# One decoder layer, its traced instructions ordered by a detailed timeline instead of a simple estimate

## Chip, core and metric

The kernel runs on one core of one Trainium2 chip. The metric is the device time of one execution in microseconds (us); the time before is the median of three runs. One more execution was profiled, and all views come from it. Engines are named as in the profile: PE (TensorE, matrix products; PEld is its loading of weights), DVE (VectorE), ACT (ScalarE), POOL (GpSimd), SP (SyncE, which here only issues DMAs).

## What is computed

One layer of a hybrid decoder in float32, for a prompt of 2048 tokens and for eight sequences of eight new tokens, each with 2048 past positions in a paged cache. The width is 1024, the hidden width of the MLP 2816.

```python
h = rmsnorm(x, norm_mix) * (1 + sc_m) + sh_m           # scales, shifts, gates from silu(c) @ w_ada
rq, rk, rv, rg, sq, sk, sv = split(h @ w_in)           # 1024 -> 3584
# 4 heads of 128, chunks of 128 tokens: retention
o = (q k^T * decay) v + (q * q_decay) s;  s = s * chunk_decay + (k * k_decay)^T v
ro = group_norm(o) * silu(rg)
# 8 heads of 64, strictly causal: stick-breaking attention
A[t, s] = sigmoid(z[t, s]) * prod_{s<j<t} (1 - sigmoid(z[t, j]));  so = rmsnorm(A v)
x = x + g_m * (concat(ro, so) @ w_out)
h = rmsnorm(x, norm_ffn) * (1 + sc_f) + sh_f
ff = (silu(causal_conv3(h @ w_up_gate)) * (h @ w_up_val)) @ w_down
x = x + g_f * ff;  y = rmsnorm(x, norm_final)
```

Outputs are also the new rows of K and V, the retention state and the state of the convolution.

## The kernel before

**Precision and tiles.** Most products are made from a high and a low part in a rounded float32 format, three products for one (`mm3`, lines 295 to 297). So each slab of weights is loaded as float32 (`raw`, two buffers of 1 MB, two slabs to a buffer), copied to its high part by ACT (line 174, `whl<-raw`) and subtracted to its low part by DVE (helper `tt`, line 159, `whl<-raw,whl`). `whl` has six buffers, that is three slabs. Activations stand in `act`, also in two parts. In PSUM there are four buffers `d` for the dense products, three buffers `z` for everything that is short, and one `acc`.

**Work by token blocks.** The prompt is cut into four blocks of 512 tokens; the 64 new tokens ride with block 0 in the projections and with block 3 in the MLP. The parts are Python generators that trace a piece of work and yield an estimate of its cost: `in_block` (normalisation and the projection by `w_in`), `decode` (attention of the new tokens over the pages), `retention`, `attention`, then per block `out_block` (projection by `w_out`) and `ffn_block`. `_weave` traces a step of the generator that is furthest behind by these estimates, so the traced program already mixes the streams: first `in_block` with `decode` and the rest of `w_ada`; then `in_block` with `retention` and the attention of block 0; then the MLPs of blocks 0 to 2 with the attention of blocks 1 to 3; last the MLP of block 3 alone. A change from one block to the next is where `out_block` waits for the block's attention and features are made for the next MLP.

**Steps of attention** (lines 1122 to 1196): `qk` multiplies queries and keys into a `z` buffer (line 1144, `z<-akk,aq`); ACT makes two sigmoids (`aom`, `abe`, lines 1147 and 1148); POOL masks or puts in the carry (lines 1151 to 1158); DVE scans along the keys (line 1161) and multiplies; five steps later `turn` transposes into a `z` buffer (line 1173, `z<-con,abe`), ACT and DVE split it (`ahl`), and a step after that `av` multiplies by the values into `acc` (line 1185). Retention makes scores (line 1015), masks them (`scd`), and its group norm reads a `z` buffer four times by ACT (line 979, `on<-z`) after a chain of small POOL instructions.

**What sets the order on the chip.** Every engine works through one queue in order, and SP issues all 1361 DMAs in one queue. Inside `TileContext` the kernel only traces. When the context closes, a list planner runs the traced instructions on a simulated machine: each time an engine of that machine is free it is given the oldest traced instruction whose inputs and buffers are ready there, and buffers are handed out as they come free there. The order so found is what is compiled, with semaphores for all dependencies. By default the machine is a simple estimate: a duration for each instruction. In the compiled program of before, the four-places-or-more moves against the traced order are 3,275 of 16,670 instructions on PE and 2,347 of 2,386 on SP. In one place the kernel holds the planner back: `tc.issue_after` keeps a page's index load behind the eighth page load before it.

## Time and profile before

| | |
|---|---|
| runs (us) | 3423.82, 3425.92, 3428.62; median 3425.92 |
| profiled execution (us) | 3422.1, of which 3420.4 from the first to the last instruction (the span) |
| mean granted clock of TensorE | 0.986 |
| moved by DMA | 527.72 MB, mean 154 GB/s |

The busy times by engine, the stages and the waits are shown in the prediction, where they are used. A wait's row names the instruction that waited and the one whose end released it, each by engine, written tile and line; a line such as 159 or 174 is that of a helper, and the tile tells which use it is. Matrix products overlap in the records, so a product's listed duration is longer than the distance to the next.

### The profile page before, as it was taken

The page shows a single profiled execution, that of the slowest core. Times are in us where ns is not written, and L with a number is a line of the kernel's source. Part 1 is how long each engine was busy: PE and PEld are TensorE (multiplying, and loading weights), DVE is VectorE, ACT ScalarE, POOL GpSimd, SP SyncE. Part 2 cuts the span into 40 slices and gives each one's busy share as a digit, 9 for nine tenths or more (in the row PEclk, how much of TensorE's full clock was granted, in tenths as well). Part 3 has the DMA queues.
Part 4 walks back from the last instruction along what each step waited for, and adds up shares of the span by engine and source line. Part 5 has one row for each costly group of instructions (what it writes and reads, how often), then busy time and mean ns, then how long its engine had stood idle before and what let it go on. Part 6 is the DMA issues. An engine that isn't in the chain of part 4 may idle for free.

```text
span 3420.4 us, 49521 instructions
## 1 busy us (share of the span) xinstructions
PE 3273.5 (96%) x17111; PEld 2676.8 (78%) x17111; DVE 2287.6 (67%) x3258; ACT 1772.8 (52%) x3153; POOL 1029.1 (30%) x1898
## 2 busy tenths in 40 slices
PE   7999999999988989999998999999899999899998
PEld 5877777776777768878877877877788787799997
DVE  5466666764665567777778777877878774554445
ACT  5457556654544446555556555555655553433223
POOL 3012001101443233433344343334433333221113
PEclk9999999999999999999999999999999999999999
DMA  6765776776656773433464343336333334332221
GB/s 235 234 202 191 235 235 209 239 241 206 198 179 193 243 224 95 126 117 113 123 199 122 117 120 108 118 113 197 118 115 108 114 105 146 106 109 81 81 87 66
DMA packets 406233, 527.72 MB, mean 154 GB/s; under 512 B 27830, under 2 KB 244009, under 8 KB 405982
## 3 DMA queue, kind: packets, MB, share of 16 engines
q1 hardware_dynamic: 405982, 524.55, 49.0%
q8 instruction: 136, 2.23, 0.3%
q14 instruction: 115, 0.94, 0.1%
HBM read 442.47 MB, written 81.99 MB: 153 GB/s over the span
## 4 chain that ended last, share of the span: by engine, by line
PE 45%; DVE 2%; POOL 1%; ACT 1%; issue 1%; DMA 1%; SPq 0%; POOLq 0%; DVEq 0%; ACTq 0%
PE d L295 11%; PE d L296 11%; PE d L297 11%; PE acc L1185 3%; PE z L1144 2%; PE z L1173 2%; PE z L297 1%; PE z L296 1%; PE z L295 1%; DVE whl L159 1%; DVE hf L159 1%; DVE aom L1161 0%; POOL ff L159 0%; ACT whl L174 0%; PE z L304 0%
## 5 line engine op out<-in xcount | busy, mean ns | idle before, releaser
L174 ACT CAST whl<-raw 128x1024 fp32r<-128x1024 f32 x456 | 477.2, 1050 | 940.9 <-PE d L296 661.7
L159 DVE TENSOR_TENSOR whl<-raw,whl 128x1024 fp32r<-128x1024 f32 x456 | 573.9, 1262 | 523.1 <-ACT whl L174 514.2
L295 PE MATMUL d<-act,whl 128*128 128x512 f32 (+2 forms) x2016 | 738.8, 367 | 2.3 <-DVE hf L159 1.4
L297 PE MATMUL d<-act,whl 128*128 128x512 f32 (+2 forms) x2016 | 734.3, 364 | 1.1 <-DVE whl L159 1.1
L296 PE MATMUL d<-act,whl 128*128 128x512 f32 (+2 forms) x2016 | 730.9, 363 | 0.2
L295 PEld LDWEIGHTS d<-act,whl 128*128 128x128 f32 x2016 | 382.7, 190 | 62.4 <-issue 3.1
L297 PEld LDWEIGHTS d<-act,whl 128*128 128x128 f32 x2016 | 382.1, 190 | 60.6 <-DVE whl L159 2.2
L296 PEld LDWEIGHTS d<-act,whl 128*128 128x128 f32 x2016 | 383.5, 190 | 55.9 <-issue 0.4
L295 PE MATMUL d<-whl,ff 128*128 128x512 f32 x704 | 279.3, 397 | 0.0
L296 PE MATMUL d<-whl,ff 128*128 128x512 f32 x704 | 278.9, 396 | 0.0
L297 PE MATMUL d<-whl,ff 128*128 128x512 f32 x704 | 278.3, 395 | 0.0
L295 PE MATMUL d<-whl,act 128*128 128x512 f32 x640 | 257.5, 408 | 5.5 <-ACT whl L174 5.5
L296 PE MATMUL d<-whl,act 128*128 128x512 f32 x640 | 258.8, 404 | 0.3 <-DVE whl L159 0.3
L1161 DVE TENSOR_TENSOR_SCAN aom<-aom,acy 128x512 f32<-128x512 f32 x192 | 256.0, 1333 | 3.1 <-ACT aom L1147 2.4
L297 PE MATMUL d<-whl,act 128*128 128x512 f32 x640 | 257.3, 403 | 0.0
L159 DVE TENSOR_TENSOR abe<-abe,aom 128x512 f32<-128x512 f32 (+2 forms) x320 | 230.1, 719 | 29.9 <-POOL abe L1151 7.9
L1185 PE MATMUL acc<-ahl,avv 128*128 128x512 f32 (+3 forms) x640 | 223.5, 411 | 18.4 <-DVE ahl L159 8.4
L1147 ACT ACTIVATE aom<-z,nb 128x512 f32<-128x512 f32 (+2 forms) x320 | 200.9, 628 | 72.6 <-PE z L1144 50.0
L1148 ACT ACTIVATE abe<-z,bb 128x512 f32<-128x512 f32 (+2 forms) x320 | 199.6, 624 | 0.0
L1144 PE MATMUL z<-akk,aq 128*128 128x512 f32 (+3 forms) x640 | 190.5, 375 | 8.6 <-DVE scd L159 5.9
L159 DVE TENSOR_TENSOR ahl<-z,ahl 128x512 fp32r<-128x512 f32 (+1 forms) x320 | 191.3, 598 | 10.3 <-ACT ahl L174 9.9
L1343 DVE SCALAR_TENSOR_TENSOR c<-a,vecs,c 128x512 f32<-128x512 f32 x176 | 133.3, 759 | 81.8 <-ACT c L1340 47.2
(295 smaller groups left out, 6238.9 us busy)
## 6 DMA issues: line engine op xcount, KB each, us to landing
raw<-in_w_in SPq DMA_DIRECT2D x56, 1024.0 KB
raw<-in_w_up_gate SPq DMA_DIRECT2D x44, 1024.0 KB
raw<-in_w_up_val SPq DMA_DIRECT2D x44, 1024.0 KB
akk<-k SPq DMA_DIRECT2D x160, 256.0 KB
page<-in_cache_k_pages SPq DMA_DIRECT2D x128, 256.0 KB
page<-in_cache_v_pages SPq DMA_DIRECT2D x128, 256.0 KB
raw<-in_w_down SPq DMA_DIRECT2D x32, 1024.0 KB
raw<-in_w_ada SPq DMA_DIRECT2D x24, 1024.0 KB
```

The costliest lines, as they stand in the source:

```text
L159: eng.tensor_tensor(o, a, b, op)
L174: act.copy(hi, src)
L295: pe.matmul(ps, sh, mh, start=start, stop=False)
L296: pe.matmul(ps, sh, ml, start=False, stop=False)
L297: pe.matmul(ps, sl, mh, start=False, stop=stop)
L1144: pe.matmul(z[:, :n], qs[g, h][:, i * P : (i + 1) * P], kk[:, c, :n], start=c == 0, stop=c == 1)
L1147: act.activation(om[:, :n], z[:, :n], AF.Sigmoid, bias=nb[:, h : h + 1], scale=-SCALE)
L1148: act.activation(be[:, :n], z[:, :n], AF.Sigmoid, bias=bb[:, h : h + 1], scale=SCALE)
L1161: dve.tensor_tensor_scan(rv, rv, rv, init, ALU.mult, ALU.bypass)
L1173: pe.transpose(ps[:, i * P : (i + 1) * P], As[u, i][:, kt * P : (kt + 1) * P], ident)
L1185: pe.matmul(accs[0][:, cs], kv[u][1][:, kt, :], m[:, cs], start=(s == g and kt == 0 and c == 0), stop=(s == 0 and kt == NT - 1 and c == 1),)
L1343: dve.scalar_tensor_tensor(c[:, :TB], a[:, j : j + TB], cw(j), c[:, :TB], ALU.mult, ALU.add)
```

## The change

One argument of the context is set. The traced program, the streams, the tiles and the buffers' counts stay as they are. The planner's simulated machine becomes the library's detailed timeline, which follows each instruction through the queue, wait and execution of its engine, and through devices that engines or DMAs share.

```diff
-    with _tile.TileContext(nc) as tc:
+    with _tile.TileContext(nc, schedule_with_timeline_sim=True) as tc:
         body(tc, ins, outs)
```

## The prediction

> **What bounds the kernel now.** I read the page first (busy times, chain of work that ended last), then cut the span into stages with the view of windows, then the waits of TensorE, and last the order of time around single stalls.
>
> ```profile
> span 3420.4 us, 49521 instructions
> PE 3273.5 (96%) x17111; PEld 2676.8 (78%) x17111; DVE 2287.6 (67%) x3258; ACT 1772.8 (52%) x3153; POOL 1029.1 (30%) x1898
> PE 45%; DVE 2%; POOL 1%; ACT 1%; issue 1%; DMA 1%; SPq 0%; POOLq 0%; DVEq 0%; ACTq 0%
> ```
>
> TensorE is the bound: busy for 3273.5 of 3420.4 us, and it heads the chain; DVE follows at 67%. A new order leaves the instructions as they are, so what it can win is the idle 146.9 us of TensorE, and what it can lose is more of the same. Where those lie, by stages (columns: stretch, its length, busy us of PE, PEld, DVE, ACT, POOL with counts, granted clock, DMA share, GB/s):
>
> ```profile
> 0.00:100.00 100.00, 79.23 (x479) 58.37 (x480) 55.49 (x70) 55.55 (x91) 26.88 (x46) 0.93 0.71 237
> 100.00:850.00 750.00, 718.50 (x3865) 572.90 (x3864) 464.94 (x704) 432.35 (x785) 100.85 (x209) 0.98 0.67 221
> 850.00:1330.00 480.00, 434.23 (x2389) 353.70 (x2389) 293.40 (x591) 236.03 (x476) 182.58 (x378) 0.98 0.64 194
> 1330.00:1780.00 450.00, 448.47 (x2121) 360.17 (x2121) 347.39 (x440) 245.51 (x418) 179.03 (x316) 1.00 0.44 130
> 1780.00:1900.00 120.00, 110.66 (x576) 89.73 (x574) 98.43 (x130) 76.56 (x143) 50.70 (x92) 1.00 0.46 140
> 1900.00:2380.00 480.00, 477.78 (x2238) 381.72 (x2237) 373.53 (x452) 260.62 (x435) 186.07 (x302) 1.00 0.42 128
> 2380.00:2480.00 100.00, 90.42 (x464) 73.53 (x463) 84.55 (x111) 64.96 (x122) 44.79 (x77) 0.97 0.39 120
> 2480.00:2880.00 400.00, 399.49 (x1868) 319.77 (x1867) 302.53 (x365) 210.68 (x339) 141.07 (x238) 1.00 0.35 105
> 2880.00:3000.00 120.00, 109.23 (x528) 90.62 (x527) 60.76 (x97) 49.58 (x100) 35.04 (x50) 0.93 0.46 151
> 3000.00:3385.00 385.00, 385.00 (x2513) 360.17 (x2512) 185.54 (x275) 128.30 (x220) 62.81 (x167) 1.00 0.27 86
> 3385.00:3420.40 35.40, 20.52 (x88) 16.12 (x87) 21.07 (x29) 12.63 (x28) 19.27 (x24) 0.84 0.18 67
> ```
>
> The reader is to see two kinds of stage. In the four long stretches of MLP (1330 to 1780, 1900 to 2380, 2480 to 2880, 3000 to 3385) TensorE idles 1.5, 2.2, 0.5 and 0.0 us: no order can win anything there. The idle time is in the start (20.8), the projections with decoding (31.5), the projections with retention and attention (45.8), the three changes from one token block to the next (9.3, 9.6, 10.8) and the end (14.9). The start and the end are chains in which nothing else is left to run, so I count them as fixed; the middle ones, 31.5 + 45.8 + 9.3 + 9.6 + 10.8 = 107.0 us, are what an order can move.
>
> **Is that idle time a matter of order?** The waits of TensorE (what waits, what it waited for: us in total, times, longest):
>
> ```profile
> PE acc L1185 <- DVE ahl L159: 8.4, 11, 2.3
> PE z L472 <- DVE c L159: 6.8, 1, 6.8
> PE acc L1185 <- ACT ahl L174: 6.7, 5, 2.5
> PE z L1144 <- DVE scd L159: 5.9, 5, 1.3
> PE z L1173 <- ACT on L979: 4.0, 3, 2.1
> PE acc L1185 <- ACT on L979: 3.0, 1, 3.0
> PE z L1015 <- ACT on L979: 3.0, 3, 1.4
> PE z L455 <- ACT on L979: 2.2, 2, 1.2
> ```
>
> Five of these rows do not name an operand. L1144 multiplies `akk` by `aq`, and `scd` is another tile, made out of the PSUM buffer that L1144 is to write; L1173, L1015 and L455 wait likewise for the group norm's `on` to have been read out of a `z` buffer, L1185 for it to leave `acc`. These are buffers that come free later than the order supposes: 5.9 + 4.0 + 3.0 + 3.0 + 2.2 = 18.1 us. One of them in order of time (start, duration, engine, line, operation; in brackets the idle time and its releaser):
>
> ```profile
> 1099.89 1.03 POOL L159 TENSOR_TENSOR rs_b<-rs_a,nhalf 128x4 f32<-128x4 f32 x1
> 1101.84 1.50 ACT L979 ACTIVATE on<-z,nm,rs_b 128x128 f32<-128x128 f32 x4 [3.63 <-POOL nm L976]
> 1103.39 0.55 PE L1173 MATMUL z<-con,abe 128*128 128x128 f32 x3 [2.12 <-ACT on L979]
> 1104.25 0.39 PE L295 MATMUL d<-act,whl 128*128 128x512 f32 x1
> 1104.48 0.39 PE L296 MATMUL d<-act,whl 128*128 128x512 f32 x1
> ```
>
> POOL's small chain and the four ACT reads hold the buffer until 1103.34; TensorE stands 2.12 us at a transpose, with dense products behind it that then start with no wait of their own. An order in which those products stood first would have filled the hole. Such an order comes from a planner that knows the chain's real duration.
>
> **The change, part by part.** It adds and removes no instruction and no DMA: the same trace of `body` is handed to the same list planner, which on each engine takes the oldest instruction that its simulated machine has ready. Only that machine's clock changes. Three things follow.
>
> (1) *Orders on PE, ACT, DVE and POOL.* The compiled program of before tells how much hangs on the machine: of 16,670 matrix instructions 3,275 stand four or more places from where they were traced. If the new clock is the better one, the five buffer waits go: 18.1 us. The two L1185 rows wait for an operand (`ahl`), the end of the path transpose, ACT, DVE, product; a better clock would put dense products ahead of part of them. The nearest bounds are all of it (8.4 + 6.7 = 15.1) and none; I take half, 7.5. The rest of the 107.0 us lies in rows of a few us each, which I cannot tell apart, and take at zero: some will go and others come. Sum: 18.1 + 7.5 = 25.6 us less.
>
> The bounds of this term: all 107.0 us less on one side. On the other the order could be worse by as much as it is now bad: the idle share of 850 to 1330 is 45.8 of 480 (9.5%); were the three changes of block and the projections with decoding (1090 us without the end stages: 750 + 120 + 100 + 120) to reach it, they would idle 103.6 instead of 61.2, 42 us more. Nothing excludes a loss, since these estimates are both only estimates.
>
> What the new clock may see that the old one may not: durations that depend on a neighbour (minimum, median, maximum in ns).
>
> ```profile
> L159 DVE TENSOR_TENSOR whl<-raw,whl x456: 1193/1225/2358, 9.1 to 3386.9; 128x1024 fp32r<-128x1024 f32 x152
> L1158 POOL COPY aom<-acy x192: 177/184/1847, 1250.6 to 2820.8; 128x1 f32<-128x1 f32 x192
> ```
>
> The same copy of one column takes 184 ns or ten times that, the same subtraction 1225 or 2358. The Trainium skill, SBUF — State Buffer, in its single rule on the shared port pair, gives a reason: a VectorE instruction with two SBUF inputs and a GpSimd instruction that reads SBUF exclude each other, and the later one blocks for the whole of the other. The trace agrees, as the copy's 1847 ns is about one such DVE instruction longer than its 184. By that rule a clock that charges the lock would also cure the other half of the L1185 waits, 7.5 us more, and the sum would be 33.1 instead of 25.6; without the lock in its model it stays at 25.6. I stay with the smaller.
>
> (2) *The order of the DMA queue.* All 1361 transfers are issued by SP, one in-order queue, and there 2,347 of 2,386 instructions stand four or more places from their traced place, so the planner decides this queue nearly alone. I cost its change at nothing, on this cover: weights are converted well ahead.
>
> ```profile
> L174 ACT CAST whl<-raw 128x1024 fp32r<-128x1024 f32 x456 | 477.2, 1050 | 940.9 <-PE d L296 661.7
> L159 DVE TENSOR_TENSOR whl<-raw,whl 128x1024 fp32r<-128x1024 f32 x456 | 573.9, 1262 | 523.1 <-ACT whl L174 514.2
> SPq L165 <- DVE whl L159: 842.1, 149, 28.9
> SPq L165 <- PE z L1144: 431.4, 80, 13.5
> SPq L165 <- PE acc L1185: 286.0, 45, 11.5
> ```
>
> ACT idles 661.7 us because TensorE has not yet finished with the old slab, which is what being ahead looks like; of the six `whl` buffers one slab (high and low part) is in use and two wait. A slab feeds 24 products (8 blocks by 3) at the pitch of the two rows at 1104 above, 0.23 us: 5.5 us. So the cover is 2 x 5.5 less one conversion (1.05 + 1.26 = 2.31): 8.7 us by which a weight load may come late.
>
> (3) *Placement of buffers and the waits that go with it* follow the order; I have no row for them and take them as part of the bounds of (1).
>
> The sum against the profiled execution: 3420.4 - 25.6 = 3394.8 us of span. That execution took 1.7 us beyond its span (3422.1), and the median of the runs lies 3.8 us above it (3425.92): 3394.8 + 5.5 = 3400 us. What is late next, where the buffer waits go: TensorE itself, since its 3273.5 us stay.
>
> **The rivals.**
>
> *Nothing to tell (0.15).* The two clocks agree where it matters, or the new one moves holes about without closing them. For it: the MLP stretches, 1715 of 3420 us, cannot move, and the old order already leaves only 4% idle. Within 0.2% (7 us, about what this kernel's measurement can tell from no change): 3419 to 3433. This includes the case in which the planner gives nearly the same order.
>
> *Slower, by the DMA queue (0.38).* If the new clock prices transfers differently, SP issues a load for attention, with its wait for a buffer, ahead of a weight load that is wanted sooner. What stands behind it is everything: SP waits 431.4 us in 80 pieces for L1144 to be done with a buffer, the longest 13.5. The point from which it decides is the cover of 8.7 us; a weight load behind the longest of those waits comes 13.5 - 8.7 = 4.8 us late, and TensorE stands for it in a stage that now idles not at all. Ten of the 228 loads (456 slabs, two to a load) in that place cost 48 us: 3425.9 + 48 = 3474. Against it: today SP makes 125 such waits, and the MLP stretches idle 4.3 us in all (1.5 + 2.2 + 0.5).
> A long stall would cost more than its length: the Trainium skill, TensorE: Matmul & The Clock Gate, Part 1, has the clock halved after some 3.4 us of idling. The granted clock of 0.93 in 2880 to 3000 beside 1.00 in the full stages agrees in sign; no run here shows the threshold.
>
> *Faster by much (within the 0.47).* Most of the 107.0 us goes, say 75: 3351. For it: the idle time comes in pieces of 1 to 3 us with dense products behind them. Against it: a planner's clock would have to be right to a microsecond after a millisecond of drift.
>
> **How the numbers follow.** Faster 0.47, because the holes read as errors of the old clock, which a better clock would correct; slower 0.38, because the streams' weights and buffer counts fit the old order and one in-order queue can undo it; within 0.2% 0.15, since 5% more or less of the idle time already leaves that band. The likeliest case has 3400, its own range 3345 (three quarters of the 107.0 gone) to 3418. The whole range goes up to 3490, the slower rival with some 13 late loads; I leave 0.05 below 3345 and 0.13 above 3490.
>
> **What would show it.** Right: TensorE's waits for `ACT on` and `DVE scd` fall from 18.1 us to a few, the stage up to the first change of block idles under 35 us, the MLP stretches stay at 99% or more, TensorE's busy time stays near 3273. Wrong: `PE d` waiting for `whl` in the MLP stretches (rival of the queue), or a change of block that idles 20 us and more instead of 10. What would make the prediction wrong is a clock that is finer but not nearer to the chip: then the holes only move, or grow.

## Result and the profile after

The changed kernel takes 3453.77 us (median of 4 runs, 3451.11 to 3455.14) against 3426.23 for the kernel before beside it: a ratio of 1.0068 with a 95% interval of 1.0055 to 1.0081, slower by 27.5 us. The prediction's likeliest case was 3400, faster, with a range up to 3490 and a chance of 0.38 on slower: the time lies inside the range, on the other side of the kernel before.

The page of the changed kernel, the span and the busy times:

```profile
span 3452.8 us, 49654 instructions
PE 3281.4 (95%) x17111; PEld 2715.3 (79%) x17111; DVE 2299.8 (67%) x3258; ACT 1778.1 (51%) x3153; POOL 1091.0 (32%) x1898
```

The span grew by 32.4 us, TensorE's listed busy time by 7.9. Before going on, the reader should see that these totals tell nearly nothing: they look like the page of before. The stages tell more. The windows of the changed kernel, cut where TensorE has done about as many products as at the cuts of before (same columns; the cut at 905 goes with 873 of before, not with 850):

```profile
0.00:100.00 100.00, 74.54 (x408) 54.29 (x409) 53.95 (x67) 53.04 (x86) 23.81 (x46) 0.86 0.69 229
100.00:905.00 805.00, 752.12 (x4033) 611.18 (x4031) 473.28 (x710) 446.62 (x809) 110.20 (x205) 0.98 0.65 210
905.00:1387.00 482.00, 428.57 (x2292) 352.80 (x2293) 290.36 (x588) 225.63 (x456) 185.81 (x383) 0.90 0.63 188
1387.00:1832.00 445.00, 445.00 (x2127) 361.90 (x2127) 353.77 (x439) 247.45 (x418) 185.34 (x314) 1.00 0.45 133
1832.00:1948.00 116.00, 110.47 (x571) 90.85 (x571) 99.96 (x131) 76.56 (x145) 54.57 (x95) 0.99 0.45 139
1948.00:2421.00 473.00, 472.97 (x2243) 383.92 (x2242) 375.00 (x454) 262.66 (x436) 187.56 (x303) 1.00 0.43 130
2421.00:2520.00 99.00, 91.52 (x464) 74.69 (x463) 84.22 (x112) 64.95 (x121) 44.03 (x77) 0.93 0.38 117
2520.00:2915.00 395.00, 394.05 (x1860) 320.21 (x1859) 300.11 (x363) 209.57 (x338) 142.37 (x234) 1.00 0.36 108
2915.00:3031.00 116.00, 106.75 (x527) 89.29 (x526) 64.66 (x101) 51.14 (x102) 42.64 (x59) 0.94 0.51 171
```

Read the lengths, not the busy shares. The start ends with 408 products done instead of 479. The MLP stretch 1387 to 1832 does 2127 products in 445 us where before needed 450 for 2121; 1948 to 2421 does 2243 in 473 (2238 in 480). The decode stage takes 805 us where before, from 100 to 873, took 773 for as many products, and TensorE idles 52.9 us in it instead of 32.4; the stage of retention and first attention takes 482 us instead of 457 (873 to 1330). So the change lost in the first part and won in the MLP part, in stretches that were listed as 99.5 to 99.7% busy before.

A finer measure for this reading: take the dense products (`whl` among the operands) in their order in both traces and compare the start of the n-th. The lag of the changed kernel behind before, in us, at four places of before's time:

| | 100 | 1400 | 2900 | 3300 |
|---|---|---|---|---|
| the change | +9.4 | +56.0 | +35.0 | +30.9 |

It loses 56 us up to the first change of block and wins 25 back after it. Inside the first part this lag swings (64 us at 900, 20 at 1100), because the two orders place the dense products differently among the others; so between 100 and 1400 it is not read for the change. It comes from one profiled execution of each kernel, and executions of one kernel differ (before took 3421.8 to 3433.6 us in one round): a few us of lag are no finding. The two halves have to be explained separately, and the experiments keep them apart.

**Where the MLP part could win.** From one and the same dense product to another (1345.1 to 2860.0 before, 1401.9 to 2895.3 after) the windows are:

```profile
1345.10:2860.00 1514.90, 1491.74 (x7100) 1197.17 (x7098) 1182.13 (x1467) 838.63 (x1426) 588.15 (x1000) 1.00 0.41 124
```
```profile
1401.90:2895.30 1493.40, 1479.41 (x7100) 1203.59 (x7099) 1189.54 (x1468) 842.61 (x1427) 600.41 (x1000) 0.99 0.42 126
```

The same 7100 products are listed as 1491.7 us busy and as 1479.4: TensorE's busy time shrank by 12 us at nearly the same clock (1.00 and 0.99). A product is listed with 0.40 us and starts 0.23 us behind the one before it, so a wait of up to 0.17 us lies inside a listed product and counts as busy. The idle time is then too small a measure, and the waits of the weight loader (PEld, which runs ahead of the product) are a better one. Its longest in these stretches, before:

```profile
PEld acc L1185 <- DVE ahl L159: 16.0, 34, 2.8
PEld z L1144 <- ACT abe L1148: 11.4, 32, 0.5
PEld acc L1185 <- ACT ahl L174: 10.5, 25, 2.9
```

and after (between the same two products):

```profile
PEld z L401 <- ACT abe L1148: 4.4, 4, 1.7
...
PEld acc L1185 <- DVE ahl L159: 2.8, 4, 1.1
PEld acc L1185 <- ACT ahl L174: 2.1, 2, 1.5
```

All listed waits of PE and PEld in this stretch together: 22.3 + 62.4 = 84.7 us before, 13.7 + 30.2 = 43.9 after; of the 41 us, 21.5 came out as time: 9.2 were listed as idle (23.2 to 14.0, most of it in the two changes of block), 12.3 lay in time listed as busy. The Trainium skill, Perfetto Trace Analysis, Identifying the Most-Contended Engine, calls the busy share of matrix products a poor measure of how near TensorE is to its limit, and names the busy share of weight loads among those to use instead. The rows agree: TensorE goes from 98.5% to 99.1%, the loader from 1197.17 of 1514.9 (79.0%) to 1203.59 of 1493.4 (80.6%).

**What changed in the first part.** From 100 us to the end of the decode stage, before (100 to 873), ScalarE at a page and the products at what is made from it:

```profile
ACT vhl L174 <- DMA page<-in_cache_v_pages: 45.0, 32, 3.8
ACT whl L174 <- DMA raw<-in_w_in: 34.8, 22, 3.9
...
PE acc L908 <- ACT vhl L174: 6.2, 9, 2.0
PE acc L908 <- DVE vhl L159: 2.1, 6, 0.7
PEld acc L908 <- ACT vhl L174: 15.4, 23, 2.4
PEld acc L908 <- DVE vhl L159: 10.4, 26, 1.0
```

after (100 to 905):

```profile
ACT vhl L174 <- DMA page<-in_cache_v_pages: 109.7, 58, 5.3
...
ACT whl L174 <- DMA raw<-in_w_in: 5.0, 3, 2.7
...
PE acc L908 <- ACT vhl L174: 17.8, 14, 2.5
PE acc L908 <- DVE vhl L159: 3.6, 6, 1.5
PEld acc L908 <- ACT vhl L174: 23.5, 17, 3.0
PEld acc L908 <- DVE vhl L159: 7.1, 12, 1.8
```

Weights now come in time (34.8 to 5.0 us), but 58 of the 128 value pages, not 32, find ScalarE standing at them, and the products' waits for `vhl` rise from 34.1 to 52.0 us. One such place in order of time, ScalarE in the changed kernel:

```profile
726.59 0.62 ACT L174 CAST vhl<-page 128x512 fp32r<-128x512 f32 x1 [5.33 <-DMA page<-in_cache_v_pages]
727.11 1.04 ACT L174 CAST whl<-raw 128x1024 fp32r<-128x1024 f32 x1
728.06 0.58 ACT L174 CAST st<-d 128x512 fp32r<-128x512 f32 x1
```

SP issued two value pages at 720.55 and 721.68; ScalarE stands idle until 726.59, and the conversion of a weight slab and the emptying of a `d` buffer are behind it in the same in-order queue. Neither waited for anything else: they start back to back once the page is in.

### The profile page after: what moved, and what is told of

The parts are those of the page before. It is cut to its first block, busy times and chain, and to the rows that moved or that the text cites. A ratio compares the mean times of both kernels' runs of the same rounds, so it can differ in the third digit from the quotient of the medians.

```text
span 3452.8 us, 49654 instructions
## 1 busy us (share of the span) xinstructions
PE 3281.4 (95%) x17111; PEld 2715.3 (79%) x17111; DVE 2299.8 (67%) x3258; ACT 1778.1 (51%) x3153; POOL 1091.0 (32%) x1898
## 4 chain that ended last, share of the span: by engine, by line
PE 57%; DVE 3%; POOL 1%; issue 1%; ACT 1%; DMA 0%; SPq 0%; POOLq 0%; ACTq 0%; DVEq 0%
PE d L295 14%; PE d L297 14%; PE d L296 14%; PE acc L1185 3%; PE z L1144 3%; PE z L1173 3%; PE z L297 1%; PE z L296 1%; PE z L295 1%; DVE hf L159 1%; DVE aom L1161 0%; DVE whl L159 0%; PE z L304 0%; PE z L305 0%; POOL rs_b L159 0%
## 5 line engine op out<-in xcount | busy, mean ns | idle before, releaser
L296 PE MATMUL d<-whl,act 128*128 128x512 f32 x640 | 255.8, 400 | 0.0
L297 PE MATMUL d<-whl,act 128*128 128x512 f32 x640 | 253.7, 397 | 0.0
L295 PE MATMUL d<-whl,act 128*128 128x512 f32 x640 | 246.6, 401 | 4.7 <-DMA act<-mx 2.5
L159 DVE TENSOR_TENSOR abe<-abe,aom 128x512 f32<-128x512 f32 (+2 forms) x320 | 237.3, 744 | 17.7 <-POOL abe L1151 1.2
L1185 PE MATMUL acc<-ahl,avv 128*128 128x512 f32 (+3 forms) x640 | 234.7, 397 | 6.6 <-DVE ahl L159 4.5
L174 ACT CAST ahl<-z 128x512 fp32r<-128x512 f32 (+1 forms) x320 | 166.8, 524 | 78.8 <-PE z L1173 69.1
```

What stands on the lines that cost most here:

```text
L159: eng.tensor_tensor(o, a, b, op)
L174: act.copy(hi, src)
L295: pe.matmul(ps, sh, mh, start=start, stop=False)
L296: pe.matmul(ps, sh, ml, start=False, stop=False)
L297: pe.matmul(ps, sl, mh, start=False, stop=stop)
L1185: pe.matmul(accs[0][:, cs], kv[u][1][:, kt, :], m[:, cs], start=(s == g and kt == 0 and c == 0), stop=(s == 0 and kt == NT - 1 and c == 1),)
```

## Experiments

Most of the runs build a program whose queues follow one planner in one part and the other planner in the other. For that, edges of order without semaphores are added between the traced instructions (the numbers come from the other compiled program); the cut between the parts is the first instruction of the first `out_block`. In short form, with the unpacking of the numbers left out:

```diff
+def _keep_order(tc, nc):
+    for nums in orders:            # one list of traced numbers for each held queue
+        for a, b in zip(nums, nums[1:]):
+            tc.add_manual_dep(traced[b], traced[a], NoSync, "kept order")
...
         body(tc, ins, outs)
+        _keep_order(tc, nc)
```

All results in one table; the ratio is to the kernel before on the same chip, the lag is that of the dense products behind before in the profiled execution, as above (which need not be the median one: e10's took 3412.1 us, e2's 3481.5).

| run | median us (range) | ratio, 95% interval | lag at 100 | 1400 | 2900 | 3300 |
|---|---|---|---|---|---|---|
| the change | 3453.77 (3451.11 to 3455.14) | 1.0068, 1.0055 to 1.0081 | 9 | 56 | 35 | 31 |
| e1 old first, new MLP | 3413.28 (3406.96 to 3415.80) | 0.9956, 0.9943 to 0.9970 | 3 | 15 | -7 | -11 |
| e2 new first, old MLP | 3474.35 (3473.25 to 3481.51) | 1.0139, 1.0116 to 1.0161 | 8 | 56 | 58 | 59 |
| e3 change, old SP first | 3541.84 (3539.99 to 3546.91) | 1.0335, 1.0311 to 1.0358 | -6 | 147 | 127 | 123 |
| e4 change, old PE first | 3454.69 (3448.81 to 3456.54) | 1.0079, 1.0054 to 1.0104 | 16 | 57 | 35 | 31 |
| e5 simple estimate, new MLP | 3413.23 (3410.93 to 3419.00) | 0.9951, 0.9935 to 0.9966 | 0 | 14 | -7 | -10 |
| e6 before, products with the values later | 3434.61 (3425.74 to 3445.06) | 1.0014, 1.0003 to 1.0026 | 0 | 7 | 9 | 11 |
| e7 change, four page buffers | 3456.10 (3454.90 to 3457.47) | 1.0075, 1.0058 to 1.0091 | 8 | 55 | 35 | 31 |
| e8 change, old ACT first | 3537.66 (3535.79 to 3541.69) | 1.0309, 1.0292 to 1.0326 | 16 | 144 | 122 | 118 |
| e10 before, steps evenly mixed | 3405.43 (3400.62 to 3412.11) | 0.9929, 0.9909 to 0.9950 | -1 | 6 | -10 | -11 |
| e11 change, old to end of decode | 3419.27 (3409.78 to 3427.79) | 0.9972, 0.9960 to 0.9984 | 3 | 22 | 1 | -2 |
| e12 change, old head | 3444.00 (3442.95 to 3449.40) | 1.0052, 1.0031 to 1.0073 | 3 | 46 | 23 | 19 |
| e13 as e10, steps cut | 3429.90 (3423.13 to 3441.09) | 1.0011, 0.9999 to 1.0023 | 0 | 25 | 9 | 1 |
| e14 before, pages cast by POOL | 3443.35 (3436.07 to 3446.85) | 1.0041, 1.0028 to 1.0054 | 0 | 17 | 19 | 21 |
| e15 change, pages cast by POOL | 3437.61 (3434.72 to 3441.41) | 1.0028, 1.0017 to 1.0040 | 9 | 36 | 16 | 12 |

### The two halves: e1 and e2

e1 is the change with all five queues held to before's order ahead of the cut; e2 is the change with them held behind it.

> The detailed timeline, but all five queues are held to the order of before for everything that is traced before the first out_block (head, projections, decoding, retention, attention of block 0); the MLP part is ordered by the timeline. Theory A (the loss lies in the first part, where the same instructions run 57 us late at 1350 us, and the MLP stretches gain: the lag shrinks to 31 us by 2950): 3426 less about 25, 3395 to 3410 us. Rival B (a full TensorE cannot gain; the lag only shrinks because a delayed stream catches up what it had in reserve): 3420 to 3432 us, the MLP stretches as long as before.

> The other way round: the timeline orders the first part, the MLP part is held to the order of before on all five queues. Theory A: the first part's loss without the MLP's gain, 3426 plus about 57, 3470 to 3490 us. Rival B: about the time of the change, 3450 to 3460 us, since the delayed stream catches up under either order.

Held to the old order, the first part loses 15 us instead of 56, and the MLP wins its 25 all the same: 3413, faster than both kernels. With the old order in the MLP part the lag stays at 56 to 59 to the end. So gain and loss belong to the two parts and don't depend on one another. The other rows of the table say the same: wherever the MLP part has the timeline's order, the lag falls by 24 to 27 us from 1400 to 3300, whatever came before it (e1, e3, e4, e5, e7, e8, e11, e12, e15).

### Is the MLP's gain order alone? e5, e6, e10, e13

e5 takes the timeline away and holds only the MLP part to its order.

```diff
-    with _tile.TileContext(nc, schedule_with_timeline_sim=True) as tc:
+    with _tile.TileContext(nc) as tc:
```

> The kernel before with its simple estimate, but from the first out block on (the four MLP stretches) every queue is held to the order that the detailed timeline gave. If the order there is the whole of the gain, the first part ends where it did before and the MLP part is 26 to 27 us shorter: 3399 us (3394 to 3405). If part of the gain comes from where the timeline puts buffers, the MLP part gains less: 3405 to 3420. If the 9 to 16 us that the first part lost in e1 belong to the held MLP order (loads of its weights issued elsewhere), they come again: 3409 to 3416.

The MLP wins 24 us, so it is the order and not where buffers lie. The total was expected at 3399 and came at 3413, the third case. The lag is 3 us at 800 and 7 at 1100, then goes to 16 at 1300: the held order has a price at the first `out_block`, where the longest listed wait in 1230 to 1376 is a load of its inputs that before does not show there:

```profile
PE d L295 <- DMA act<-mx: 6.0, 1, 6.0
```

e6 tests the plainest reason, that the product with the values stands too close behind the split of its `ahl`.

```diff
-            if 6 <= t < total + 6:
-                av(*divmod(t - 6, 4))
+            if 7 <= t < total + 7:
+                av(*divmod(t - 7, 4))
```

> The kernel before with one edit in the attention groups: the product of each group with the values stands one step further behind its scores (t-7 in place of t-6), the simple estimate as before. If the MLP stretches lost time to products issued in the moment in which their operand became ready (116 of 537 within 0.3 us of it, the weight loads' waits for ahl 26.5 us), most of that goes: 3404 to 3416 us. If a TensorE that is listed as 99.6% busy has nothing to win, 3422 to 3430. If the later product holds the ah buffers one step longer and the split behind waits for them, 3430 to 3445.

This failed as a cure and is the more useful for it. Of 537 such products before, 116 started within 0.3 us of the end of their operand's split, in e6 1 of 538; the old waits are gone. But others stand in their place:

```profile
PEld z L1144 <- ACT abe L1148: 17.8, 34, 3.2
PEld z L1144 <- DVE ahl L159: 9.5, 25, 1.2
```

All listed waits of PE and PEld in the stretch sum to 82.4 us (84.7 before), and the stretch takes 1517.5 us (1514.9). Here the step moved as a block, and its wait moved to the `z` buffers of the scores; only waits that disappear from the sum are won.

e10 mixes the traced program finer, still with the simple estimate: the attention stream may take a step after every three dense products, no longer only after a whole piece of the MLP (5.2 units of cost, some 24 products). `since` holds the cost of the dense products since the MLP's last yield, 0.65 for each three.

```diff
     def mm3(ps, s, m, start, stop):
...
+        for p in pumps:
+            p()
...
+        def pump():
+            since[:] = [mlp.got, since[1] + 0.65 if since[0] == mlp.got else 0.65]
+            while att.live and att.got / att.total < (mlp.got + since[1]) / mlp.total:
+                if not att.step():
+                    break
```

> As e9, but a step of attention stays in one piece: only the distance between steps is made even (13 dense products ahead of a product with the values, before 65). If even spacing of the steps is what counts, as e9: 3402 to 3412 us. If what counts is work between a step's transposes, its products with the values and its scores, nothing is won: 3420 to 3435.

The stretch falls to 1499.2 us (7092 products in it instead of 7100), the waits to 18.6 + 35.7 = 54.3, the kernel to 3405.4: 0.7% below before, the best of all that ran. The other expectation, that work between the parts of a step is what counts, did not hold; the even spacing of whole steps gives 15.7 of the 21.5 us.

e13 cuts the step as well. So does e9, but there the step's cost also became 2.1 instead of 1.3 and retention's 0.5 instead of 1.3, so that attention fell behind the MLP (its dense products run 57 us ahead of before at 2900 and 172 behind at 3300): 3594.39 us, ratio 1.0482, which says nothing on the question.

```diff
                 turn(*divmod(t - 5, 4))
+                yield 0.4
...
                 av(*divmod(t - 6, 4))
+                yield 0.4
...
-            yield 1.3
+            yield 0.5
```

> The kernel before with its simple estimate; in the MLP stretches the traced program itself is mixed finer: after every three dense products the attention stream may take a step, and a step is cut in three (transposes; products with the values; scores), so that dense products come between the parts of a step (a dense product ahead of a product with the values 163 times in the compiled program, before 65, the change 210). If the gain of the MLP stretches is this mixing alone, the listed waits of TensorE and its weight loader there fall from 85 us to some 45 and the time to 3402 to 3412 us. If only the timeline's knowledge of when an operand is ready gives it, 3420 to 3432. If the finer mixing brings waits of its own for z buffers (as in e6), 3432 or more.

> As e10, with the step of attention cut in three of 0.4, 0.4 and 0.5 (in e9 the step's cost had become 2.1 by an edit at the wrong place, so that attention fell behind, and retention's cost 0.5). If dense products between the parts of a step add to the even spacing of e10, the listed waits fall to some 45 us and the time to 3393 to 3403 us. If the even spacing is all, as e10: 3403 to 3412. If the cut brings waits for z buffers, 3415 or more.

In the MLP stretch e13 about equals e10: 1499.7 us (with 18 fewer products in it), listed waits 53.2. Cutting the steps adds nothing there. What it lost, 25 us by 1400, it lost ahead of this stretch (the cut also changed the first attention group); that was not followed further. The remaining 6 us between e10 and the timeline's order are not explained.

### Where the first part loses: e11, e12, e3, e4, e8

e12 holds all queues to the old order for the first 100 us, e11 to the end of the decode stage.

> The change with every queue held to the order of before in the first 100 us alone. If the lag adds up place by place, the 9 us lost there come back and no more: 3441 to 3448 us. If the decode stage is bound by its own chain and swallows them, 3449 to 3458. If the early load of w_in in the head (issued at 12 us in place of 35) is what puts the decode stage out of step, 3400 to 3430.

> The change with every queue held to the order of before up to the end of the decode stage (some 870 us), the stage of retention and first attention placed by the timeline. If the decode stage is where the order loses, this gives back nearly all that e1 gave back: 3408 to 3422 us. If the stage behind it (900 to 1350 us, with 29 us busy of 50 at a clock of 0.60 in one slice) loses on its own account, 3430 to 3448.

With e1, the lag at 1400 can be taken apart: 56.0 for the change, 45.6 with the old head, 22.4 with old head and decode, 14.6 with all of it old. So the head costs 10, the decode stage 23, the stage of retention and first attention 8, and 15 stay, as in e5 (14), that come with the MLP's order and not with the first part's. 10 + 23 + 8 + 15 - 25 = 31, the lag at the end. The medians of whole runs agree: 3453.8, 3444.0, 3419.3 and 3413.3 differ by 9.8, 24.7 and 6.0. Only for the middle step do the intervals not overlap.

Holding a single queue was to name the engine.

> The change, with SP's queue alone held to the order of before in the first part. If the DMA order makes the loss (the rival of the prediction): most of the 57 us of the first part come back, 3400 to 3415 us. If the compute engines' order makes it: 3445 to 3460 us.

> The change, with TensorE's queue alone held to the order of before in the first part. If the order of TensorE makes the loss (projections taken ahead of decoding, so that decoding, which ends the stage, comes late): 3400 to 3420 us. If TensorE's order only follows what ACT, DVE or the loads do late: 3440 us or more, with waits of TensorE for vhl and page as in the change or longer.

> The change with ScalarE's queue held to the order of the kernel before up to the first out block; every other queue is placed by the timeline. If ScalarE's order there makes the loss (value casts too early, 107 us of waits for pages), the decode stage ends 30 to 48 us earlier: 3405 to 3425 us. If ScalarE's order is no more the cause than TensorE's was, 3447 to 3460. If the old ScalarE order stands across the new loads as the old load order stood across the new work, 3480 or more.

With TensorE's old order (e4) the lag is the same, so its order alone does not bring the time back. The products' waits for `vhl` fall to 10.5 us there, but others stand in their place (35.1 us for `aT` from DVE), and ScalarE still stands 95.9 us at pages: the products' waits at `vhl` are not themselves the loss. e3 and e8 say less than I had hoped. The loads alone or ScalarE alone in the old order, across queues of the new one, lose about 145 us by 1400 where the change loses 56: there the queues of one plan fit together, and half a plan is worse than either whole one. A gain by TensorE's old order could be hidden in e4 in the same way.

Part of what the first part loses is work at a lower granted clock, some 10 us in all and some 6 of the 23 in the decode stage; the rows are in the last section.

### ScalarE at the page: e7, e14, e15

> The change with four page buffers in place of three in the decode stage, and nine aT in place of ten to make room. If the 48 us that the decode stage lost come from casts of value pages placed on ScalarE before their page can arrive, a fourth buffer lets loads start a page earlier: the waits of ScalarE for pages fall from 107 to 50 us or less and the time to 3405 to 3430 us. If the loads' start isn't what the casts wait for (they wait for the round trip of a load that the queue issued late), 3447 to 3460. If nine aT hold the scores up, 3465 or more.

```diff
-                dict(smp=1, page=3, khl=2, vhl=3, aT=10, qsm=1, ksm=1, oT=1,
+                dict(smp=1, page=4, khl=2, vhl=3, aT=9, qsm=1, ksm=1, oT=1,
```

A fourth buffer, with nine `aT` to make room, won no time (3456.1). ScalarE's standing at value pages fell from 109.7 to 89.1 us, so a fifth of it went without any gain. e14 and e15 leave order and buffers to each planner and take the page's cast off ScalarE:

```diff
-                split(vh[:, 0], vh[:, 1], page(pages_v, b, n, "page"))
+                pg = page(pages_v, b, n, "page")
+                pool.tensor_copy(vh[:, 0], pg)
+                tt(dve, vh[:, 1], pg, f(vh[:, 0]), ALU.subtract)
```

> Control for e15: the kernel before, with the high part of each value page copied by POOL in place of ScalarE (128 copies of 128x512; ScalarE's took 0.62 us each, POOL's rows of that size 1.3 to 1.5 us with two inputs). In the old order ScalarE waited 45 us for these pages and TensorE's listed idle is small there: 3418 to 3432 us on every theory; above 3440 if POOL's copies are too slow for the products.

> The change, with the high part of each value page copied by POOL in place of ScalarE, so that ScalarE no longer stands at a page that has not come (107 us in the changed kernel), and what is queued behind it goes on. If that standing is what the decode stage lost its 25 us to, the time falls by 15 to 30 us against the change: 3425 to 3440 us. If the order loses through many small waits on all engines alike, 3447 to 3460, or as far above 3454 as e14 stands above 3426. If the timeline makes another order altogether, its lag by stage tells more than its time.

e14 in its decode stage (100 to 890):

```profile
POOL vhl L899 <- DMA page<-in_cache_v_pages: 180.0, 61, 9.3
PE acc L910 <- POOL vhl L899: 7.7, 9, 2.1
PE acc L910 <- DVE vhl L159: 2.8, 8, 0.5
PEld acc L910 <- POOL vhl L899: 13.0, 15, 2.4
PEld acc L910 <- DVE vhl L159: 11.7, 25, 0.9
```

e15, same window:

```profile
POOL vhl L899 <- DMA page<-in_cache_v_pages: 209.5, 62, 11.9
PE acc L910 <- POOL vhl L899: 6.3, 7, 1.6
PE acc L910 <- DVE vhl L159: 3.6, 6, 0.8
PEld acc L910 <- POOL vhl L899: 9.2, 9, 2.1
PEld acc L910 <- DVE vhl L159: 5.3, 6, 1.3
```

The standing at pages is still there, even longer, but now in POOL's queue, which has little else to do. The products' waits for `vhl` are 35.2 us in the old order and 24.4 in the new, where with ScalarE they were 34.1 and 52.0. In time: the change with the cast on POOL takes 3437.6 us, 16 us less than with it on ScalarE (ratios 1.0028 and 1.0068, intervals apart), and its lag at 1400 falls from 56.0 to 35.8, by 20 us. The control, the old order, lost 15 us by the same move (3427.9 to 3443.4; lag at 1400 17.0). So against its own control the change adds 18.8 us at 1400 instead of 56.0, and in the whole time it is no longer slower (3437.6 and 3443.4, intervals 1.0017 to 1.0040 and 1.0028 to 1.0054, which overlap).

So the cast of value pages on ScalarE accounts for about 20 of the 41 us that the first part's own order loses (10 + 23 + 8). It is 37 (56.0 less 18.8) only if POOL's cast costs the change as much as it costs the control, which was not tried. That the reason is the standing, with what is queued behind it, is argued from the rows: e15 also takes 128 casts of 0.62 us off ScalarE, and in the control that won nothing. Two things remain open. The timeline makes another order altogether once the cast has moved, so that more than the cast differs between the change and e15. And no run shows why the timeline puts casts ahead of their pages. A price for page loads that is too low would do it, but no run changed that price.

## Why the prediction was wrong

Three steps failed. The first two gave the wrong sign: the first part's own order lost 41 us, where the sum had nothing but gains. The third hid a gain.

- *Term (2), the DMA queue at nothing, with a cover of 8.7 us.* The cover holds for weight slabs, and in the MLP stretches of the changed kernel TensorE indeed does not wait for weights. It was counted for weights alone. Page loads in the decode stage have no such cover, and the engine that stands at them is ScalarE, whose queue also converts the weights and empties `d`. That the waits of an engine that is busy for 52% of the span can hold up the others is what the term left out: ScalarE's waits for value pages grew from 45.0 to 109.7 us, and at 726.59 in the rows shown, 5.33 us of standing hold two other streams. The decode stage lost 23 us; moving the cast gave 20 back (under an order that differs in more than the cast). Whether loads come later or casts earlier than before was not separated.
- *The start, of which the prediction says "I count them as fixed" together with the end.* The start is not fixed: at 100 us the changed kernel has done 408 products instead of 479, and the old order in the first 100 us alone (e12) gives 10 us back.
- *"No order can win anything there"* (the four MLP stretches). It took 99.7% busy as full. From 1345 to 2860 the waits of PE and PEld sum to 85 us; half of them went, and 21.5 us of time with them, 12 of which the windows had listed as busy. The rows that said so stood in the view of waits under PEld, which I had not used: 16.0 and 10.5 us for `ahl` alone.
- *Term (1), buffer waits and half of the `ahl` waits, 25.6 us.* The waits went about as said, but did not bring the time. In the changed kernel:

```profile
PE acc L1185 <- DVE ahl L159: 4.5, 6, 1.7
...
PE acc L1185 <- ACT ahl L174: 2.0, 2, 1.3
...
PE z L1173 <- ACT on L979: 0.4, 1, 0.4
```

  The five buffer rows fell from 18.1 to 0.4 us (waits for `scd` and `on` at other lines come to 4.9), the `ahl` pair from 15.1 to 6.5, and the idle time of the three changes of block from 29.7 to 5.5 + 7.5 + 9.3 = 22.3. That the total of the gain in the MLP part (25) is near the 25.6 is chance: the five buffer rows lie in the stage of retention (850 to 1330), which as a whole became longer (482 us instead of 457, 53.4 of them idle, where I expected under 35).
- *The rival "slower, by the DMA queue"* had the sign and, within its price (3474), the size, but the wrong place: a weight load late in the MLP. What was late was a page in decoding. Its price of 48 us came from ten late weight loads, so the nearness of the size is luck.
- *The bound of a loss, 42 us, taken from the worst stage,* was just wide enough, by luck: the first part's own order lost 10 + 23 + 8 = 41 us, but 10 of them in the start, which the bound left out, and 15 more came with the MLP's order.
- *"A long stall would cost more than its length":* at the end of the decode stage the granted clock stood at half for 21 us of nearly unbroken work; the rows are below.

## What to carry to other kernels

A matrix engine that is listed as busy is not thereby full: before writing a stretch off, sum the waits of its weight loader there, and after an edit check that the sum fell and did not only move (e6). In an in-order queue a load that comes late also holds whatever stands behind the instruction that waits for it (ScalarE at 726.59), so look at what is queued behind a conversion of data that arrives at uncertain times. Moving it to an engine with less to do won 16 us under the new order here and lost 15 under the old one: it has to be tried with the order that will run. And a planner's gain can be cut out of its loss: hold each stage to the better order, or write the better mixing into the traced program, as e10 did with the plain estimate (3405 us against 3428 for before beside it).

## What the hardware showed that was not expected

At the end of the decode stage the changed kernel has little to fill in, and TensorE ran short chains: from 903 to 906 it was busy for 0.39 us. Then its granted clock fell to half (3 us windows; the clock is the third value from the right):

```profile
903.00:906.00 3.00, 0.39 (x3) 0.17 (x3) 1.14 (x3) 0.02 (x1) 1.40 (x5) 1.00 0.74 252
906.00:909.00 3.00, 0.66 (x3) 0.47 (x3) 0.66 (x3) 0.70 (x3) 1.19 (x4) 0.59 0.37 120
```

A wait of 6.93 us for a load followed, at half the clock already:

```profile
923.13 0.45 PE L1090 MATMUL z<-sqT,skT 128*64 128x64 f32 x2 [6.93 <-DMA skT<-rks]
```

And the clock stayed there while TensorE was at work again almost without a gap:

```profile
941.00:944.00 3.00, 3.00 (x11) 2.35 (x11) 1.42 (x2) 2.21 (x4) 1.20 (x2) 0.50 0.63 170
944.00:947.00 3.00, 1.09 (x8) 0.59 (x6) 2.65 (x6) 0.00 (x0) 2.56 (x5) 0.99 0.78 235
```

The Trainium skill, TensorE: Matmul & The Clock Gate, Part 1, has the clock halved after some 3.4 us of idling and full again after as long a time of steady work. The fall agrees, if 0.39 us of work in 3 us counts as idling; the return doesn't: from 923 to 944 TensorE is listed as busy for 20.5 of 21 us, and every window of 3 us there stands at 0.50. Many of these products use only 64 of the 128 rows or columns. In the kernel before the same products ran among others at a clock of 1.00 (868 to 907). Whether alone they are too little to raise the clock was not tried.

What this costs can be read from two of these lines, the same instructions in both kernels (860 to 1000). Before:

```profile
L1104 PE MATMUL acc<-rmh,km 128*64 128x128 f32 x64 | 8.1, 277 | 0.0
L1113 PE MATMUL z<-scd,skm 64*128 64x512 f32 x16 | 7.9, 615 | 0.1
```

After:

```profile
L1113 PE MATMUL z<-scd,skm 64*128 64x512 f32 x16 | 13.0, 956 | 1.4 <-DVE skm L1096 1.4
L1104 PE MATMUL acc<-rmh,km 128*64 128x128 f32 x64 | 12.7, 369 | 0.2 <-DMA rmh<-in_state_ret 0.2
```

They take 25.7 us instead of 16.0. With the old head (e12) they take 23.5, with the old order to the end of decoding (e11) 17.9 and with all of the first part old (e1) 16.0, so some 6 of these 10 us lie within the 23 of the decode stage. With the cast on POOL (e15) they still take 26.6: what e15 gives back is something else. In the stage 905 to 1387 the mean clock was 0.90 (0.97 before, 873 to 1345); what that cost beyond these two lines no run shows.

POOL's cast of a 128x512 page took 0.62 us in the median, as long as ScalarE's (0.62), and not the 1.3 to 1.6 us of its rows with two inputs; its mean was 0.79, since some took up to 1.72. That engine was a far nearer substitute than the rows of the trace suggested, though the control still paid 15 us for it.
